# Block products: sums of weight blocks made one product sooner

## The chip, the cores and the metric

The kernel runs on one core of one Trainium2 chip. A core has five engines that work side by side, each through its own queue in order: TensorE (PE, matrix products; its weight loads are listed apart as PEld), VectorE (DVE), ScalarE (ACT), GpSimd (POOL) and SyncE (SP, which here only issues transfers). An engine that must wait for another stops at that instruction, and all behind it in its queue waits too. The metric is device time in microseconds, as the median of several executions; less is better.

## The reference, cut to what matters

One layer of a hybrid decoder: a feed-forward, a mixer (sparse attention beside a gated recurrence), a second feed-forward, and a final normalisation. 512 tokens, model width 1024, hidden width 2816, all in float32. The change concerns the two feed-forwards:

```python
def rmsnorm(x, g):
    y = x32 * lax.rsqrt(jnp.mean(x32 * x32, axis=-1, keepdims=True) + EPS)
    return (y * g.astype(jnp.float32)).astype(x.dtype)

def swiglu(x, w_gate, w_up, w_down):
    return (jax.nn.silu(x @ w_gate) * (x @ w_up)) @ w_down

x = x + 0.5 * swiglu(rmsnorm(x, ffn1_norm[l]), ffn1_wg[l], ffn1_wu[l], ffn1_wd[l])
...
x = x + 0.5 * swiglu(rmsnorm(x, ffn2_norm[l]), ffn2_wg[l], ffn2_wu[l], ffn2_wd[l])
```

## The kernel before, in words

**Number format.** A float32 operand is split into an upper half h (ACT rounds it by a copy to the type fp32r) and a lower half l (DVE subtracts h from the operand). A product of two split operands is three matmuls: h·h, h·l and l·h. For weights these tiles are called wh and wl, for hidden tiles hh and hl.

**Feed-forward.** `ffn_up` (L380) computes the gate and up projections of 22 hidden tiles of 128 rows. In the first feed-forward two tiles are done ahead of it and n0 is 2, in the second n0 is 0. The next DIRECT = 4 tiles (L47) are computed plainly, so that f0 = n0 + 4 hidden tiles come out before the block products: 6 in feed-forward 1, 4 in feed-forward 2.

**Block products.** The remaining tiles go in pairs. Two hidden tiles of one projection and the halves of the input and of the tokens form a 2x2 block product, done with seven half-size products instead of eight (a scheme of the Strassen kind). One such pair for one projection is called w here: there are count = 16 of them in feed-forward 1 and 18 in feed-forward 2; even w is the gate, odd w the up projection. The seven products need these weights: two halves of the tile x (products 1 and 2), a22 (4), s1 (5), s3 (7), and two sums that DVE makes: s2 = s1 + the first half of x (product 6), and s4 = s2 + the second half of x (product 3). s1 and s3 are themselves made by transfers: SyncE loads one block, and GpSimd issues a second transfer that adds another block to it (L444 to L451).

**The stream.** `stream` (L453 to L458) lists all products in the order in which PE runs them: 1 and 2 of w, 4 of w-1, 6 of w, 3 of w-1, 5 and 7 of w. It has 112 entries in feed-forward 1 and 126 in feed-forward 2. The order is written out by hand. For each product i the loop at L560 to L574 does this:

- `products(i)`: 12 matmuls on PE, each 128x256, that add into a PSUM tile. Products 1, 6, 7 and 4 of one w add to the same tile, beta, one after the other;
- `results(i - 1)`: after product 1, 6 and 7 ACT copies beta's present contents out to SBUF (tiles t1 and t2, shown as tg for the gate and tu for the up projection), and PE may go on adding to beta only then. DVE and ACT combine the parts into hidden tiles h;
- `prepare(i + 4)`: four products ahead (LEAD, L46), the weights of that product are made ready: the sum if it is product 6 or 3, then ACT's rounding (wh), then DVE's subtraction (wl). A pair of tiles wh, wl holds two products; there are three pairs;
- once in 14 products, while i // 14 < f0, `halve` (L577) splits one of the earlier hidden tiles into hh and hl for the down projection;
- once in 7 products, `load` (L436) asks for the weights of a later w; the raw tile x has three buffers, the blocks s1, s3, a22 and the sums s2, s4 come from 60 slots.

The first four products are made ready before the loop, while the plain tiles are computed (L543 to L545). Instructions that belong to a manual schedule keep this order; at its end the scheduler may mix in the first instructions of the down projection `ffn_down` (L584), whose order it chooses itself.

In the profile every instruction has the line of a helper (L174, or L162 for transfers), so that groups are told apart by their tiles. A product's matmuls read "cm" tiles (the prepared input) and wh or wl.

Of the kernel before, what the change touches and what calls it, by code (L numbers as in the profile page):

```python
# [10 lines left out]
F32R = mybir.dt.float32r  # L11
# [3 lines left out]
P = 128  # L15
# [30 lines left out]
LEAD = 4  # L46
# [133 lines left out]
def hybrid_kernel(ctx, tc, xt, vec, w1u, w1d, wm, wki, wrg, watt, wrnn, wout, w2u, w2d, out):  # L180
# [11 lines left out]
    wsp = ctx.enter_context(tc.tile_pool(name="wsp", bufs=3))  # L192
# [9 lines left out]
    def nm(s):  # L202
        cnt[0] += 1
        return f"{s}_{cnt[0]}"

    def slot(dt=F32, name="s"):
        return plan.take("slot", big.tile([P, S], dt, tag="slot", name=nm(name)))
# [7 lines left out]
    def psum(tag="mm"):  # L215
        return psp.tile([P, S], F32, tag=tag, name=nm(tag))
# [15 lines left out]
    WMAX = KD * P  # L232
# [6 lines left out]
    def wsplit(r, h, l):  # L239
        A.activation(h, r, AF.Copy)  # L240
        V.tensor_sub(l, r, f(h))

    def wload(src, cols):
        r, h, l = wtiles(cols)
        Q.dma_start(r, src)
        wsplit(r, h, l)
        return h, l
# [132 lines left out]
    def ffn_up(y, wu, n0, hs, g, waiting=(), given=()):  # L380
# [7 lines left out]
        H = KD // 2 * P  # L388
        f0 = n0 + DIRECT
        count = KF - f0  # L390
        ws = []
# [61 lines left out]
        stream = []  # L453
# [3 lines left out]
        w = count - 1  # L457
        stream[-3:] = [(5, w), (7, w), (3, w - 1), (4, w), (3, w)]  # L458
        units = []

        def prepare(i):
            p, w = stream[i]
            o = ws[w]
            if i % 2 == 0:
                units.append([wsp.tile([P, WMAX], F32R, tag=t, name=nm(t)) for t in ("wh", "wl")])
            h, l = (t[:, i % 2 * H:(i % 2 + 1) * H] for t in units[i // 2])
            if p == 6:
                o.s2 = slot(F32, "s2")
                V.tensor_add(o.s2, o.s1, o.x[:, :H])
            if p == 3:  # L470
                o.s4 = slot(F32, "s4")
                V.tensor_add(o.s4, o.s2, o.x[:, H:])
            wsplit({1: lambda: o.x[:, :H], 2: lambda: o.x[:, H:], 6: lambda: o.s2, 5: lambda: o.s1, 7: lambda: o.s3,
                    4: lambda: o.a22, 3: lambda: o.s4}[p](), h, l)

# [51 lines left out]
        with tc.manual_schedule(engines=ENGINES):  # L527
# [4 lines left out]
            for d, (n, j) in enumerate(direct):  # L532
                sums.append(psum(("aux", "mm")[n % 2]))
                if d == 1:
                    norm_rest(norm)
                    hs.extend(ffn_act(*p) for p in waiting)
                gemm(sums[d], split_[d], y, range(KD), last=False, upto=KD // 2)
                steps = [results_direct(d - 1)] if d else []
                if d + 2 < len(direct):
                    together(prepare_direct(), *steps)  # L540
                    fetch()
                else:
                    together(*steps)  # L543
                    for i in range(2):
                        prepare(2 * (d + 2 - len(direct)) + i)  # L545
                if d == 0:
                    for _ in range(3):
                        next(norm)
                if d in (4, 6):
                    load_ = load(len(ws))  # L550
                if d >= 4:
                    next(load_, None)
                if d > 1:
                    next(operands, None)
                gemm(sums[d], split_[d], y, range(KD), first=False, since=KD // 2)
                if d > 1:
                    next(operands, None)
            for _ in operands:
                pass
            for i in range(len(stream)):  # L560
                products(i)
                if i:
                    results(i - 1)
                else:
                    together(results_direct(len(direct) - 1))
                if i + LEAD < len(stream):
                    prepare(i + LEAD)
                else:
                    halve(hs, f0 + i + LEAD - len(stream))
                if i % 14 == 12 and i // 14 < f0:  # L570
                    halve(hs, i // 14)
                if i % 7 == 1 and len(ws) < count:
                    load_ = load(len(ws))
                next(load_, None)  # L574
# [61 lines left out]
    def given(r):  # L636
        h, l = (wsp.tile([P, WMAX], F32R, tag=t, name=nm(t)) for t in ("wh", "wl"))
        wsplit(r, h, l)
        return h, l
# [10 lines left out]
    pu, w = psum(), given(AH[0])  # L650
# [673 lines left out]
    for a, b in CHUNKS[:-1]:  # L1324
        w = wload(w2d[n, :, a * P:b * P], (b - a) * P)
# [3 lines left out]
    w = wload(w2d[n, :, a * P:b * P], (b - a) * P)  # L1329
# [32 lines left out]
    o = {}  # L1362
# [75 lines left out]
```

## Time and profile before

| What | us |
|---|---|
| median of 3 runs | 1103.74 (1102.88 to 1103.88) |
| the profiled execution | 1102.85 |
| its span, first to last instruction | 1101.1 |
| PE busy | 1081.7 |
| PE weight loads busy | 948.2 |
| DVE busy | 764.5 |
| ACT busy | 596.1 |
| POOL busy | 100.7 |

The stream of feed-forward 1 lies at about 73 to 238 us of the span, its down projection behind it to about 363; the mixer goes to about 734; the stream of feed-forward 2 lies at about 783 to 966. PE's granted clock is 0.995 of full speed over the span.

How to read the lines: an instruction is written as output tile <- input tiles, with shapes; a row of the timeline gives its start, its length, and in brackets how long its engine was idle before it and what ended that idle time. "A <- B: t, n, m" in the view of waits means that A waited t us in total for B, in n places, m at the longest. The chain that ended last is followed back from the last instruction of the program, at each step to what released it or to the instruction before it on its engine. "s" stands for a tile s1, s2, s3 or s4, since buffer numbers are left out.

### The profile page before, as it was taken

The page shows a single profiled execution, that of the slowest core. Times are in us where ns is not written, and L with a number is a line of the kernel's source. Part 1 is how long each engine was busy: PE and PEld are TensorE (multiplying, and loading weights), DVE is VectorE, ACT ScalarE, POOL GpSimd, SP SyncE. Part 2 cuts the span into 40 slices and gives each one's busy share as a digit, 9 for nine tenths or more (in the row PEclk, how much of TensorE's full clock was granted, in tenths as well). Part 3 has the DMA queues.
Part 4 walks back from the last instruction along what each step waited for, and adds up shares of the span by engine and source line. Part 5 has one row for each costly group of instructions (what it writes and reads, how often), then busy time and mean ns, then how long its engine had stood idle before and what let it go on. Part 6 is the DMA issues. An engine that isn't in the chain of part 4 may idle for free.

```text
span 1101.1 us, 16405 instructions
## 1 busy us (share of the span) xinstructions
PE 1081.7 (98%) x6184; PEld 948.2 (86%) x6184; DVE 764.5 (69%) x1376; ACT 596.1 (54%) x1093; POOL 100.7 (9%) x121
## 2 busy tenths in 40 slices
PE   9999999999999999999999999999999999999995
PEld 7889999998888777888888888888999999988885
DVE  6687777785333778999799868556877777773333
ACT  6665555564222558968885664346655555552220
POOL 0151111100000000000000000003411111000001
PEclk9999999999999999999999999999999999999998
DMA  7396677733333342232232203336967776543322
GB/s 269 83 242 183 159 180 194 162 106 102 102 90 102 116 134 81 83 98 85 77 96 83 81 30 99 112 115 155 218 156 190 191 159 179 122 133 93 96 63 77
DMA packets 61135, 140.22 MB, mean 127 GB/s; under 512 B 7168, under 2 KB 16512, under 8 KB 61056
## 3 DMA queue, kind: packets, MB, share of 16 engines
q1 hardware_dynamic: 45936, 116.58, 33.8%
q0 software_dynamic: 14976, 22.55, 13.4%
q8 instruction: 48, 0.79, 0.3%
q14 instruction: 31, 0.25, 0.1%
q10 hardware_dynamic: 144, 0.05, 0.0%
HBM read 130.24 MB, written 2.10 MB: 120 GB/s over the span
## 4 chain that ended last, share of the span: by engine, by line
PE 79%; DVE 9%; ACT 6%; DMA 3%; issue 3%; SPq 0%; DVEq 0%; ACTq 0%
PE mm L174 55%; PE aux L174 24%; DVE wl L174 3%; ACT wh L174 3%; DVE s L174 1%; DMA a<-w1u 1%; DMA gr<-wrg 1%; DVE tg L174 1%; ACT hh L174 1%; DVE yl L174 1%; ACT tg L174 0%; SPq L162 0%; DVE yf L174 0%; DMA wr<-w1u 0%; ACT cm L174 0%
## 5 line engine op out<-in xcount | busy, mean ns | idle before, releaser
L174 DVE TENSOR_TENSOR wl<-wr,wh 128x1024 fp32r<-128x1024 f32 (+3 forms) x204 | 193.0, 955 | 115.4 <-ACT wh L174 115.0
L174 ACT ACTIVATE wh<-wr 128x1024 fp32r<-128x1024 f32 (+4 forms) x206 | 171.2, 835 | 177.7 <-PE mm L174 67.1
L174 PE MATMUL mm<-cm,wh 128*128 128x256 f32 x1088 | 200.4, 284 | 2.5 <-ACT tg L174 2.5
L174 PEld LDWEIGHTS mm<-cm,wh 128*128 128x128 f32 x1088 | 169.7, 192 | 4.9 <-ACT tg L174 4.8
L174 PE MATMUL mm<-yh,wh 128*128 128x512 f32 (+1 forms) x416 | 164.7, 397 | 1.4 <-ACT yh L174 0.6
L174 PE MATMUL mm<-yl,wh 128*128 128x512 f32 (+1 forms) x416 | 163.3, 393 | 0.8 <-DVE yl L174 0.8
L174 PE MATMUL mm<-yh,wl 128*128 128x512 f32 x408 | 159.9, 392 | 0.0
L174 PE MATMUL mm<-cm,wl 128*128 128x256 f32 x544 | 153.9, 283 | 0.0
L174 PE MATMUL aux<-cm,wh 128*128 128x256 f32 x816 | 150.0, 283 | 0.0
L174 ACT ACTIVATE wh<-s 128x512 fp32r<-128x512 f32 x136 | 81.9, 626 | 101.7 <-DVE s L174 69.9
L174 DVE TENSOR_TENSOR wl<-s,wh 128x512 fp32r<-128x512 f32 x136 | 93.7, 690 | 52.9 <-ACT wh L174 50.6
L174 PEld LDWEIGHTS aux<-cm,wh 128*128 128x128 f32 x816 | 127.3, 192 | 0.0
L174 PE MATMUL aux<-cm,wl 128*128 128x256 f32 x408 | 115.5, 283 | 0.0
L174 PEld LDWEIGHTS mm<-cm,wl 128*128 128x128 f32 x544 | 104.3, 192 | 0.0
L174 PEld LDWEIGHTS mm<-yh,wh 128*128 128x128 f32 (+1 forms) x416 | 78.3, 188 | 19.2 <-ACT yh L174 1.9
L174 PEld LDWEIGHTS mm<-yl,wh 128*128 128x128 f32 (+1 forms) x416 | 78.0, 187 | 17.3 <-DVE yl L174 2.2
L174 PEld LDWEIGHTS mm<-yh,wl 128*128 128x128 f32 x408 | 77.0, 189 | 16.6 <-DVE wl L174 0.3
L174 PE MATMUL mm<-hh,wh 128*128 128x512 f32 (+1 forms) x206 | 78.8, 382 | 0.0
L174 PE MATMUL mm<-hl,wh 128*128 128x512 f32 (+1 forms) x206 | 78.5, 381 | 0.0
L174 PE MATMUL mm<-hh,wl 128*128 128x512 f32 (+1 forms) x206 | 78.4, 381 | 0.0
L174 PEld LDWEIGHTS aux<-cm,wl 128*128 128x128 f32 x408 | 78.3, 192 | 0.0
L174 PE MATMUL aux<-hh,wl 128*128 128x512 f32 x154 | 60.0, 390 | 0.0
(207 smaller groups left out, 1893.3 us busy)
## 6 DMA issues: line engine op xcount, KB each, us to landing
wr<-wm SPq DMA_DIRECT2D x39, 512.0 KB, 3.6
wr<-w2u SPq DMA_DIRECT2D x26, 512.0 KB, 3.7
wr<-w1u SPq DMA_DIRECT2D x21, 512.0 KB, 4.6
s<-w2u SPq DMA_DIRECT2D x36, 256.0 KB, 4.6
s<-w2u POOLq DMA_DIRECT2D x36, 256.0 KB, 5.4
s<-w1u SPq DMA_DIRECT2D x32, 256.0 KB, 5.1
s<-w1u POOLq DMA_DIRECT2D x32, 256.0 KB, 5.4
wr<-w1d SPq DMA_DIRECT2D x16, 448.0 KB, 3.3
```

The source lines that it names most:

```text
L174: return call(*args, **kw)
```

## The change

`prepare` made the sum for product 6 or 3 in the same step in which it also rounds and subtracts it. Now a function of its own, `add_weights`, makes it, and `prepare(i)` calls it for product i + 1, ahead of product i's own rounding and subtraction. The first LEAD = 4 products keep their sums where they were. On DVE the sum thus moves from just before its own subtraction to just before the subtraction of the product in front; between the two places lie the results of one product. The tile of the sum is taken from the slots one product sooner. The stream, the transfers as the program lists them and the number of instructions stay.

```diff
-        def prepare(i):
-            p, w = stream[i]
+        def add_weights(i):
+            p, w = stream[i] if i < len(stream) else (0, 0)
             o = ws[w]
-            if i % 2 == 0:
-                units.append([wsp.tile([P, WMAX], F32R, tag=t, name=nm(t)) for t in ("wh", "wl")])
-            h, l = (t[:, i % 2 * H:(i % 2 + 1) * H] for t in units[i // 2])
             if p == 6:
                 o.s2 = slot(F32, "s2")
                 V.tensor_add(o.s2, o.s1, o.x[:, :H])
             if p == 3:
                 o.s4 = slot(F32, "s4")
                 V.tensor_add(o.s4, o.s2, o.x[:, H:])
+
+        def prepare(i):
+            if i < LEAD:
+                add_weights(i)
+            if i + 1 >= LEAD:
+                add_weights(i + 1)
+            p, w = stream[i]
+            o = ws[w]
+            if i % 2 == 0:
+                units.append([wsp.tile([P, WMAX], F32R, tag=t, name=nm(t)) for t in ("wh", "wl")])
+            h, l = (t[:, i % 2 * H:(i % 2 + 1) * H] for t in units[i // 2])
             wsplit({1: lambda: o.x[:, :H], 2: lambda: o.x[:, H:], 6: lambda: o.s2, 5: lambda: o.s1, 7: lambda: o.s3,
                     4: lambda: o.a22, 3: lambda: o.s4}[p](), h, l)
```

## The prediction, made before the changed kernel was run

> **What bounds the kernel now.** I began with the page's busy table, then took the waits, the chain that ended last, and the timelines of ScalarE (ACT), VectorE (DVE) and TensorE (PE) around one repeating wait.
>
> ```profile
> span 1101.1 us, 16405 instructions
> PE 1081.7 (98%) x6184; PEld 948.2 (86%) x6184; DVE 764.5 (69%) x1376; ACT 596.1 (54%) x1093; POOL 100.7 (9%) x121
> ```
>
> TensorE is the bound, and 19.4 us of the span are left in which it does nothing. The change touches only the product streams of the two feed-forwards, so I looked for what PE waits for there.
>
> ```profile
> PEld mm L174 <- ACT tg L174: 4.8, 11, 0.4
> ...
> PE mm L174 <- ACT tg L174: 2.5, 11, 0.2
> ACT wh L174 <- DVE s L174: 69.9, 53, 2.9
> ```
>
> PE waits 11 times for one kind of ACT instruction, the copy of a partial result out of PSUM ("tg"). ACT waits much longer, 69.9 us, for DVE's sums of weight blocks ("s"), which is what the change moves. Whether the second feeds the first is shown by the whole chain, and then by the same view cut to one place. The columns are start, length, what.
>
> ```profile
> 76.58 1.69 PE mm L174 x12
> ...
> 95.77 1.70 PE mm L174 x12
> ...
> 116.42 1.70 PE mm L174 x12
> ...
> 199.02 1.70 PE mm L174 x12
> ...
> 210.80 2.88 PE aux L174 x24
> ...
> 220.88 2.88 PE aux L174 x24
> ...
> 805.03 1.70 PE mm L174 x12
> ...
> 866.97 1.70 PE mm L174 x12
> ```
>
> ```profile
> 93.52 0.69 DVE s L174
> ...
> 94.30 0.15 ACT wh L174
> ...
> 94.83 0.62 ACT hh L174
> 95.45 0.28 ACT tg L174
> ```
>
> Undisturbed, seven products take 220.88 - 210.80 = 10.08 us, so one product (12 matmuls) takes 1.44 and fourteen take 20.16. The rows of 1.70 us stand 116.42 - 95.77 = 20.65 apart. Each therefore costs 0.49 us. From 95.77 to 199.02 there are (199.02 - 95.77) / 20.65 = 5 steps, that is 6 such places in feed-forward 1. From 805.03 to 866.97 there are 3 steps, 4 places in feed-forward 2. These are exactly the iterations in which an earlier hidden tile is also halved ("hh", every 14 products, for f0 = 6 and 4 tiles). The eleventh wait, at 76.58, is the third product of feed-forward 1. The short chain names the cause: sum, rounding of the sum (wh), rounding of the hidden tile (hh), and only then the copy that PE needs.
>
> ACT and DVE at the first place:
>
> ```profile
> 88.94 0.63 ACT L174 ACTIVATE tg<-tg 128x512 f32<-128x512 f32 x1 [1.09 <-DVE tg L174]
> 89.48 0.62 ACT L174 ACTIVATE wh<-a 128x512 fp32r<-128x512 f32 x1
> 91.45 0.63 ACT L174 ACTIVATE wh<-s 128x512 fp32r<-128x512 f32 x1 [1.36 <-DVE s L174]
> 91.99 0.37 ACT L174 ACTIVATE tu<-mm 128x256 f32<-128x256 f32 x1
> 94.30 0.63 ACT L174 ACTIVATE wh<-s 128x512 fp32r<-128x512 f32 x1 [1.94 <-DVE s L174]
> 94.83 0.62 ACT L174 ACTIVATE hh<-h 128x512 fp32r<-128x512 f32 x1
> 95.36 0.37 ACT L174 ACTIVATE tg<-mm 128x256 f32<-128x256 f32 x1
> ```
>
> ```profile
> 88.49 0.42 DVE L174 SCALAR_TENSOR_TENSOR tg<-aux,tg 128x256 f32<-128x256 f32 x1
> 90.12 0.69 DVE L174 TENSOR_TENSOR wl<-a,wh 128x512 fp32r<-128x512 f32 x1 [1.22 <-ACT wh L174]
> 90.73 0.69 DVE L174 TENSOR_TENSOR s<-s,wr 128x512 f32<-128x512 f32 x1
> 92.12 0.69 DVE L174 TENSOR_TENSOR wl<-s,wh 128x512 fp32r<-128x512 f32 x1 [0.70 <-ACT wh L174]
> 92.73 0.42 DVE L174 TENSOR_TENSOR tu<-aux,tu 128x256 f32<-128x256 f32 x1
> 93.18 0.43 DVE L174 TENSOR_TENSOR h<-tu,tg 128x256 f32<-128x256 f32 x1
> 93.52 0.68 DVE L174 TENSOR_TENSOR s<-s,wr 128x512 f32<-128x512 f32 x1
> ```
>
> ```profile
> 95.26 0.28 PE L174 MATMUL mm<-cm,wl 128*128 128x256 f32 x1
> 95.77 0.50 PE L174 MATMUL mm<-cm,wh 128*128 128x256 f32 x2 [0.23 <-ACT tg L174]
> ```
>
> Products are numbered from 0, as in the code; the one at 95.77 is 15. Matmuls start 0.12 apart (1.44 / 12), so it was due at 95.38. Counting back, product 14 began at 93.94, 13 at 92.50, 12 at 91.06. A product's last matmul runs 0.28, so its result is there 0.16 after the next one begins: 11's at 91.22, 12's at 92.66. The copy at 95.36 reads product 12, so it could have run 2.7 us sooner. It stood behind wh and hh, which stood behind the sum at 93.52, which stood behind DVE's wait for ACT at 92.12. The two engines take turns waiting for each other.
>
> **The change, part by part.**
>
> *The moved sums.* There are 2 x 16 in feed-forward 1 and 2 x 18 in feed-forward 2. One in each lies among the first four products and stays, so 66 move and none is added. At 0.68 us each, 45 us of DVE work change place. I replay the rows above with the new order. In the iteration of product 10 the first sum now follows the row at 88.49: 88.85 to 89.5, while DVE waits for ACT anyway (1.22 idle before 90.12), so "wl<-a" stays at 90.12 and the sum costs nothing. Without that cover it would put 0.6 us (90.73 to 90.12) on all DVE work behind it. ACT rounds the sum right behind "wh<-a", at about 90.0 instead of 91.45. DVE makes the second sum at 90.73, the lower half at 91.35, tu at 91.95, h at 92.4. ACT copies tu at 91.26 when product 11 is out, rounds the second sum at 91.55 (it is there at about 91.4), hh at 92.1, and the copy tg follows product 12 at 92.7. It ends near 93.1. PE needs it at 95.38, so 2.3 us are in hand and the wait goes. What is late next on ACT is only the result of PE itself.
>
> *Sum.* 10 waits x 0.49 = 4.9 us. The eleventh stays: the copy at its head comes in the first iterations, ahead of any moved sum.
>
> *Two other readings of the same waits.* The matmul row gives 10/11 of 2.5 = 2.3 us, the weight loads' row 10/11 of 4.8 = 4.4 us. The distance of starts is the measure with nothing modelled in it, and I take 4.9. The Trainium skill, Perfetto Trace Analysis, section "Identifying the Most-Contended Engine", says that matmul busy time is a bad measure of TensorE's headroom because pipelined instructions look smaller in the trace, and that weight-load busy time should be used. By the one row the time would be 1101.4, by the other 1099.3; the trace agrees with the page, since 4.4 is near the 4.9 of the starts and 2.3 is not.
>
> *Sums wait for an accumulating transfer one product sooner.*
>
> ```profile
> s<-w1u POOLq DMA_DIRECT2D x32, 256.0 KB, 5.4
> ```
>
> ```profile
> 70.96 2.11 POOL L162 DMA_DIRECT2D s<-w1u  x2
> ```
>
> ```profile
> 79.85 0.69 DVE L174 TENSOR_TENSOR s<-s,wr 128x512 f32<-128x512 f32 x1
> ```
>
> The tightest is the first moved sum, at 79.85, where DVE was not idle; it would now start near 79.0. Its transfer was issued from 70.96 and lands 5.4 later at the median, 76.4. If it landed only at 79.85, DVE would stand 0.9 us once, and the product behind it (the eighth, begun near 76.58 + 5 x 1.44 = 83.8) would still have its weights. I take 0.
>
> *Buffers.* The raw tile is read for the last time by the second sum, so SyncE may issue the next loads about 1.4 us sooner. PE waits for no DMA in the streams, so that gains nothing; GpSimd's accumulating loads follow them and get sooner too. The slots of s2 and s4 are taken one product sooner out of 60. In the order of the instructions no late new releaser shows; I take 0.
>
> *The seam to the down projection.* The scheduler orders the last iterations anew: on DVE and ACT the first three splits of down weights come after one or two other instructions, and PE runs the first output tile for 16 matmuls straight where five matmuls of the second tile stood.
>
> ```profile
> 239.17 1.22 DVE L174 TENSOR_TENSOR wl<-wr,wh 128x1024 fp32r<-128x1024 f32 x1 [0.79 <-ACT wh L174]
> ...
> 246.03 0.69 DVE L174 TENSOR_TENSOR hl<-h,hh 128x512 fp32r<-128x512 f32 x1
> ```
>
> ```profile
> 246.18 0.39 PE L174 MATMUL aux<-hh,wh 128*128 128x512 f32 x1
> ```
>
> The lower half of 246.03 is done at 246.72; it would be needed 0.23 (one matmul) after 246.18, so PE would wait 0.3 us, and perhaps 0.7 again a few tiles on, if DVE were no sooner: 1.0 per feed-forward, 2.0 in all. Against it, DVE idles 0.79 before 239.17 and ACT's part of that comes from a late sum, so both should be over 0.8 us earlier. In the other direction, PE has no gap here to gain. I take 0 and keep 2.0 for the range.
>
> **The sum** against the profiled execution: 1102.85 (span 1101.1 and 1.75 around it) less 4.9 is 1097.95. The median of the runs, 1103.74, is 0.89 above that execution, so I forecast 1103.74 - 4.9 = 1098.8.
>
> **Rivals.**
>
> *Half.* The matmul row is right, or the copy stays late in some places: 2.3 us, 1101.4. For it: PE's own idle time. Against it: the step of 20.65. Chance 0.06.
>
> *No change: the gap is one of buffers.* The split weights have three pairs of buffers, and a regular gap could be the wait for one; then sums made sooner wait for their buffer instead: 1103.7. Against it: "wh<-s" at 94.30 takes the buffer of products 10 and 11, and "tu<-mm" at 91.99 already read product 11, so the buffer was free 2.3 us before. The Trainium skill, the same page, section "Optimization Strategy", says that the same gap repeating can mean too little SBUF or PSUM for the next tile; by that rule this rival holds, and the trace disagrees. Chance 0.04.
>
> *Slower: the sum ahead of the subtraction.* On DVE each moved sum now stands in front of the lower half of an earlier product. Where DVE does not wait for ACT, that half and all behind it are 0.6 us late, and at a product boundary PE pays 0.49 as above. It decides once the lower halves are ready less than 0.6 us ahead of PE. Here "wl<-a" ends at 90.81 for product 14, begun at 93.94: 3.1 us in hand. If it came in each of the 33 weight pairs it would cost 33 x 0.49 = 16.2, less 4.9: 1115.0. Chance 0.06.
>
> *The seam loses* its 2.0: 1100.8, chance 0.04. The forecast has 0.80.
>
> **How the numbers follow.** A run of this kernel can tell about 0.2% (2.2 us) from no change. Faster by more than that: forecast, seam and half of "half", 0.87; within it, 0.07; slower, 0.06. The range goes from 1097.7 (0.9 below for the spread of the runs, 1102.88 to 1103.88, and for the eleventh wait) to 1101.5 (the seam's bound and "half"), which leaves out the last two signs, about 1 in 10.
>
> **What would show it.** In the profile after, PE's wait for "ACT tg" should count 1 instead of 11; starts fourteen products apart should be 20.16 apart in both streams; ACT's wait for "DVE s" should fall from 69.9 to under 10, and in its place ACT waits for PE; DVE's busy time should stay at 764. The forecast is wrong if new PE waits for "DVE wl" appear in the streams, or gaps after about 243 and 970 at the seams.

## The result, and the profile after

| | before | changed |
|---|---|---|
| median, us | 1103.06 (1102.27 to 1103.88, 5 runs) | 1097.68 (1096.5 to 1098.07, 5 runs) |
| ratio to before | 1 | 0.9949, 95% interval 0.9935 to 0.9962 |
| span of the profiled execution, us | 1101.1 | 1096.2 |

The changed kernel is faster by 5.4 us in the medians and by 4.9 us between the two profiled executions. The forecast was 4.9 us, and 1098.8 us with a range that began at 1097.7. The ratios here and below, with their 95% intervals, are worked out from all executions and are not exactly the quotients of the medians.

The view of waits of the changed kernel, its lines for PE first, then ACT's wait for the sums:

```profile
PE aux L174 <- ACT rl L174: 1.7, 2, 1.1
PE aux L174 <- DVE last L174: 1.5, 1, 1.5
PE aux L174 <- DVE cc L174: 1.1, 1, 1.1
PE mm L174 <- DVE yl L174: 0.8, 2, 0.6
...
PE aux L174 <- DMA cm<-cb: 0.2, 1, 0.2
```

```profile
ACT wh L174 <- DVE s L174: 30.9, 17, 2.0
```

PE no longer waits for "ACT tg"; the 11 places are gone, and one wait for a transfer has come at the head of a stream. ACT waits 30.9 us for sums instead of 69.9. The whole chain (start, length, what) shows where the time went:

```profile
24.18 5.01 PE mm L174 x22
...
70.54 5.84 DMA cm<-cb
76.94 1.45 PE mm L174 x12
...
94.23 2.88 PE mm L174 x24
97.11 2.88 PE aux L174 x24
...
117.27 2.88 PE aux L174 x24
...
235.35 11.81 PE mm L174 x52
...
737.82 9.79 PE aux L174 x48
...
961.79 11.81 PE mm L174 x52
...
1089.26 1.58 DVE o L174 x4
```

117.27 - 97.11 = 20.16: fourteen products now take what fourteen undisturbed products took before. The same points in the whole chain of before:

```profile
24.06 5.01 PE mm L174 x22
...
238.16 8.19 PE mm L174 x36
...
740.79 9.77 PE aux L174 x48
...
966.59 6.23 PE mm L174 x27
...
1094.13 1.58 DVE o L174 x4
```

By stage: up to the end of the first stream 214.10 against 211.17, 2.93 gained (6 x 0.49 = 2.94 was forecast); the down projection and the mixer 0.16; up to the end of the second stream 225.80 against 223.97, 1.83 gained (4 x 0.49 = 1.96); the rest 0.07; the start gave back 0.12. The sum is 4.87. PE's granted clock reads 1.00 in both streams of both profiles, and fourteen undisturbed products take the same 20.16 us in both, so the clock has no part in what the streams gained.

The timelines of ACT and DVE at the place that the prediction replayed; all times stand 0.12 later here:

```profile
89.60 0.62 ACT L174 ACTIVATE wh<-a 128x512 fp32r<-128x512 f32 x1
90.12 0.62 ACT L174 ACTIVATE wh<-s 128x512 fp32r<-128x512 f32 x1
91.39 0.38 ACT L174 ACTIVATE tu<-mm 128x256 f32<-128x256 f32 x1 [0.65 <-PE mm L174]
91.67 0.62 ACT L174 ACTIVATE wh<-s 128x512 fp32r<-128x512 f32 x1
92.19 0.62 ACT L174 ACTIVATE hh<-h 128x512 fp32r<-128x512 f32 x1
92.83 0.38 ACT L174 ACTIVATE tg<-mm 128x256 f32<-128x256 f32 x1
```

```profile
88.94 0.68 DVE L174 TENSOR_TENSOR s<-s,wr 128x512 f32<-128x512 f32 x1
90.25 0.69 DVE L174 TENSOR_TENSOR wl<-a,wh 128x512 fp32r<-128x512 f32 x1 [0.62 <-ACT wh L174]
90.86 0.68 DVE L174 TENSOR_TENSOR s<-s,wr 128x512 f32<-128x512 f32 x1
91.46 0.68 DVE L174 TENSOR_TENSOR wl<-s,wh 128x512 fp32r<-128x512 f32 x1
```

The copy tg starts at 92.83 instead of 95.36. The sum at 88.94 fills part of DVE's wait for ACT (0.62 left of 1.22), and "wl<-a" is as early as before, 90.25 against 90.12 + 0.12.

### The profile page after: what moved, and what is told of

Same layout as the page of the kernel before. It is cut to its first block, busy times and chain, and to the rows that moved or that the text cites. A ratio compares the mean times of both kernels' runs of the same rounds, so it can differ in the third digit from the quotient of the medians.

```text
span 1096.2 us, 16417 instructions
## 1 busy us (share of the span) xinstructions
PE 1079.5 (98%) x6184; PEld 948.4 (87%) x6184; DVE 763.6 (70%) x1376; ACT 598.8 (55%) x1093; POOL 100.6 (9%) x121
## 4 chain that ended last, share of the span: by engine, by line
PE 88%; DVE 6%; ACT 3%; issue 1%; DMA 1%; SPq 0%; DVEq 0%; ACTq 0%; POOLq 0%
PE mm L174 60%; PE aux L174 29%; DVE wl L174 1%; ACT wh L174 1%; DVE yl L174 1%; DMA cm<-cb 1%; ACT L174 0%; DVE yf L174 0%; DVE ca L174 0%; DMA x<-xt 0%; DVE xc L174 0%; ACT rl L174 0%; DVE h L174 0%; DVE o L174 0%; ACT yh L174 0%
## 5 line engine op out<-in xcount | busy, mean ns | idle before, releaser
L174 ACT ACTIVATE wh<-s 128x512 fp32r<-128x512 f32 x136 | 83.0, 623 | 38.9 <-DVE s L174 30.9
L174 PE MATMUL aux<-hl,wh 128*128 128x512 f32 x154 | 60.0, 389 | 0.0
```

The source lines that it names most:

```text
L174: return call(*args, **kw)
```

## The experiments

Theory: the gain is ten PE waits of 0.49 us. Each comes from one chain, at the ten places where two iterations in a row each make a sum and the second also rounds a hidden tile: DVE and ACT alternate, and the copy that PE needs stands behind them. Rivals: the gain is spread over the moved sums; the sums ahead of the subtractions cost something; the half microsecond beyond 4.9 is a second gain.

All kernels ran in 5 rounds beside the kernel before (4 to 11 executions of each), whose medians there were 1102.42 us (first four) and 1102.74 us (last four). The variants of the changed kernel replace the test on LEAD by a condition:

```diff
+        def sooner(j):
+            return LEAD <= j < len(stream) and CONDITION
...
-            if i < LEAD:
+            if not sooner(i):
                 add_weights(i)
-            if i + 1 >= LEAD:
+            if sooner(i + 1):
                 add_weights(i + 1)
```

**The changed kernel again** (no edit).

> The changed kernel once more beside the kernel before. Theory: ten waits of 0.49 us and nothing else, 4.9 us, a ratio of 0.9956; the half microsecond that the first measurement gave beyond that (5.4 us, 0.9949) is scatter of the runs, and the profiled spans differ by 4.9. Rival: another 0.5 us or more is really gained elsewhere; then the ratio stays at 0.995 or below and the span falls by more than 5.3.

1097.98 us, ratio 0.9964 (0.9951 to 0.9978), span 1096.2. The gain is 4.4 us here and was 5.4 in the first measurement; 4.9 lies in both intervals, and the span is the same. Nothing speaks for a second gain.

**All sums but those of the ten places.**

```diff
+            CONDITION: not ((j - LEAD) % 14 in (11, 12) and (j - LEAD) // 14 < f0)
```

> All sums sooner except the two (s2 and s4) of each of the ten halving iterations: 46 of 66 moved. Theory: the chain sum, rounding, rounding of the hidden tile, copy is whole again in each of the ten places; PE waits 10 or 11 times for the copy, and the time is that of the kernel before (ratio 1.000). Rival (the gain is spread over all moved sums): 46/66 of 5.4 us, 3.8 us, ratio 0.9966.

1103.22 us, ratio 1.0005 (0.9997 to 1.0014). The waits in its profile:

```profile
PE mm L174 <- ACT tg L174: 2.3, 10, 0.2
...
PEld mm L174 <- ACT tg L174: 4.3, 10, 0.4
```

With 46 of the 66 sums moved nothing is gained, and PE waits ten times for the copy. The gain lies in those ten places.

**Only ten sums.**

```diff
+            CONDITION: (j - LEAD) % 14 == 12 and (j - LEAD) // 14 < f0
```

> Only ten sums sooner: s4 in each of the ten halving iterations. Theory, replayed from the rows of before at the first place: the second sum at 90.7, the first at 91.4, its rounding at 92.1, the copy tu at 92.6, the rounding of the second sum at 92.9, the hidden tile at 93.4, the copy tg ends near 94.3; PE needs it at 95.38, so the wait goes and the whole 4.9 us are gained (ratio 0.9956). Rival (spread): 10/66 of 5.4 us, 0.8 us, ratio 0.9993.

1098.04 us, ratio 0.9962 (0.9950 to 0.9975): the whole gain from 10 of 66 sums. PE's one wait for the copy that is left is the one at the third product of feed-forward 1. The view of waits has ACT waiting longer for the sums than before the change, at no cost:

```profile
PE mm L174 <- ACT tg L174: 0.2, 1, 0.2
```

```profile
ACT wh L174 <- DVE s L174: 79.2, 54, 2.9
```

The replay had the two sums in the wrong order. s2 stands first here, and ACT rounds it while DVE makes s4. The copy tg started at 92.91, or 93.3 on the clock of before, whose stream began 0.41 later; I had it at 93.9.

**The halving moved, no sum moved.** This is an edit of the kernel before.

```diff
-                if i % 14 == 12 and i // 14 < f0:
-                    halve(hs, i // 14)
+                if i % 14 == 0 and 0 < i // 14 <= f0:
+                    halve(hs, i // 14 - 1)
```

> The kernel before with no sum moved; the halving of a hidden tile stands two iterations later in each period of 14, where no sum is made. Theory: without the 0.5 us of the hidden tile's rounding ahead of it the copy starts at about 94.8 and ends at 95.2, before PE needs it at 95.38; at the new place ACT has no copy to make, so PE does not wait and 4.9 us are gained (ratio 0.9956), perhaps 0.5 less if the margin of 0.2 us does not hold everywhere. Rival (it is the sums themselves that hold PE): nothing is gained, ratio 1.000.

1097.38 us, ratio 0.9960 (0.9948 to 0.9972). The same gain without touching a sum. ACT at the first place (its stream began 0.35 earlier than that of before), and ACT's wait for the sums:

```profile
93.97 0.63 ACT L174 ACTIVATE wh<-s 128x512 fp32r<-128x512 f32 x1 [1.94 <-DVE s L174]
94.51 0.36 ACT L174 ACTIVATE tg<-mm 128x256 f32<-128x256 f32 x1
```

```profile
ACT wh L174 <- DVE s L174: 105.8, 64, 3.3
```

The rounding still waits 1.94 us for the sum, but nothing stands between it and the copy, and that is enough: the copy ends at 94.87, or 95.22 on the clock of before, and PE needs it at 95.38. ACT's total wait for sums is half as large again as before, and the time is as good as the best. In these kernels the size of that wait says nothing of the time.

**Only s2, only s4.**

```diff
+            CONDITION (s2): stream[j][0] == 6
+            CONDITION (s4): stream[j][0] == 3
```

> Only the sums s2 (product 6) sooner, 32 of 66. Theory: s2 ahead shortens the alternation of the two engines before s4, so the whole gain comes from it alone: replayed, s4 at 92.4, its rounding at 93.1, the hidden tile at 93.7, the copy ends near 94.5, 0.9 before PE needs it; ratio 0.996. Rival (each half of the sums carries its share): 32/66 of the gain, ratio 0.998.

> Only the sums s4 (product 3) sooner, 34 of 66. Theory: the whole gain again, as the ten s4 alone gave it; ratio 0.996. Rival (shares): ratio 0.998.

1098.36 us, 0.9961 (0.9947 to 0.9974), and 1098.21 us, 0.9958 (0.9945 to 0.9970). Each half of the change gives all of it. The gain is no sum of shares: the chain need only be shortened once, by more than the 0.5 us that PE waited.

**Moved sums made twice and three times.** The result stays the same; N is 2 or 3.

```diff
-                V.tensor_add(o.s2, o.s1, o.x[:, :H])
+                for _ in range(N if i >= LEAD else 1):
+                    V.tensor_add(o.s2, o.s1, o.x[:, :H])
```

(and so for s4)

> The changed kernel with each moved sum made twice, the second writing the same result: 66 sums of 0.6 us more on DVE, 40 us in all. It prices the rival 'the sum ahead of the subtraction'. Theory: DVE has 165 - 129 = 36 us idle in the stream of feed-forward 1 and takes 31 x 0.6 = 19 more; the subtraction and the copy come 0.6 to 1.2 us later and 2.3 us are in hand; no PE wait, time that of the changed kernel (ratio 0.996). Rival: lower halves late at the 33 pairs, up to 16 us more, ratio 1.011.

> Each moved sum made three times: 132 sums of 0.6 us more, 79 us. Theory: in the stream of feed-forward 1 DVE would have 129 + 37 = 166 us of work for 161 us of PE, so DVE becomes the bound there and PE waits for wl; a loss of 3 to 10 us per stream against the changed kernel, ratio 1.002 to 1.015. Rival: still hidden, ratio 0.996.

Twice: 1097.94 us, ratio 0.9956 (0.9943 to 0.9968), nothing lost. ACT there, first place; its stream lies about 0.8 later than that of before (its first matmul starts at 74.10 against 73.34):

```profile
93.01 0.63 ACT L174 ACTIVATE wh<-s 128x512 fp32r<-128x512 f32 x1 [0.61 <-DVE s L174]
93.54 0.62 ACT L174 ACTIVATE hh<-h 128x512 fp32r<-128x512 f32 x1
94.06 0.36 ACT L174 ACTIVATE tg<-mm 128x256 f32<-128x256 f32 x1
```

The copy ends at 94.42 and PE starts product 15 at 96.13, with no wait, so 1.7 us are left of the changed kernel's margin of 2.3. Three times: 1124.74 us, ratio 1.0202 (1.0188 to 1.0216), a loss of 27 us against the changed kernel; I had expected 6 to 20. Waits, and one of the places on PE:

```profile
PE mm L174 <- ACT tu L174: 21.5, 16, 1.7
```

```profile
108.42 0.50 PE L174 MATMUL mm<-cm,wh 128*128 128x256 f32 x2 [1.66 <-ACT tu L174]
130.50 0.51 PE L174 MATMUL mm<-cm,wh 128*128 128x256 f32 x2 [1.67 <-ACT tu L174]
```

DVE at that place, ahead of the wait:

```profile
101.40 2.14 DVE L174 TENSOR_TENSOR s<-s,wr 128x512 f32<-128x512 f32 x3
103.45 0.68 DVE L174 TENSOR_TENSOR wl<-a,wh 128x512 fp32r<-128x512 f32 x1
104.05 2.14 DVE L174 TENSOR_TENSOR s<-s,wr 128x512 f32<-128x512 f32 x3
106.11 0.68 DVE L174 TENSOR_TENSOR wl<-s,wh 128x512 fp32r<-128x512 f32 x1
106.71 0.42 DVE L174 TENSOR_TENSOR tg<-aux,tg 128x256 f32<-128x256 f32 x1
```

What the rival "the sum ahead of the subtraction" feared, DVE work that comes too late for PE, thus does come, but only between one and two extra sums for each moved one. That DVE would be the bound was right: in those 22.08 us (130.50 - 108.42) it is busy for 20.64, and the chain that ended last runs mostly along its sums and lower halves there. But PE does not wait for the lower halves (wl), as I wrote: it is once more the copy out of PSUM that it waits for, behind ACT, behind DVE, in 16 places, one in 14 products. The step there is 22.08 us against 20.16 in the ten periods in which a hidden tile is also halved; later in feed-forward 2 it is 21.47. This run adds work to DVE and does not test the order of the same work.

## Where the prediction was right, and the terms that failed

*What bounds, and the sum.* Right. 10 x 0.49 = 4.9 against 4.87 between the profiles, stage by stage. The median fell by 5.4 in the first measurement and by 4.4 in the second; the five other kernels in which these waits are gone and nothing new came lie 4.4 to 5.0 below the kernel before (0.9956 to 0.9962). The mechanism is the one that was forecast.

*How the numbers follow.* This is the step that failed: the two terms that turn the gain into a time, the base and the spread. 1097.68 lies 0.02 us below 1097.7, the lower end, and 1.16 below the forecast. Of that, 0.68 is the base: the forecast started from 1103.74, the median of three executions, which with five is 1103.06 (and beside the experiments 1102.42 and 1102.74). The other 0.48 is the gain in the medians, 5.38 against 4.9, which the repeat, with 4.4, does not confirm. The prediction had a nearer base: the one profiled execution, 1102.85, gave it 1097.95. The spread was too small as well. 0.9 came from those three executions, between 1102.88 and 1103.88, while the same changed program ran between 1096.34 and 1099.25 in ten; and the lower end stands only 1.1 below the forecast, so about 0.2 is left for the eleventh wait, which by the distance of starts is 0.44 (78.10 - 74.78 = 3.32 for two products that undisturbed take 2.88). Either term alone, put right, would have held the result; that it missed by 0.02 and not by more, or not at all, is chance.

What makes one execution of the same program 2.9 us longer than another was not tried. The runs show what it goes with: the spans of the ten are 1096.2 to 1097.4 us at a mean granted clock of 0.994, 1095.9 to 1096.2 at 0.995, 1094.7 to 1095.5 at 0.996, and 1094.6 at 0.997. Between the clock and the time no cause is shown.

*The other readings.* The matmul row (2.3) was wrong, the weight loads' row (4.4) and the distance of starts (4.9) near. The Trainium skill, Perfetto Trace Analysis, section "Identifying the Most-Contended Engine", says this of busy shares, that the matmul row is a poor measure of the headroom and the weight loads' row a better one. Carried over to these waits, the trace agrees: 4.87 was gained.

*The moved sums.* The replay of the first place was right to 0.05 us (copy at 92.83 - 0.12 = 92.71 against 92.7). That ACT's wait for sums would fall under 10 us was wrong: it is 30.9, in 17 places of up to 2.0. Fifteen of them, of 1.98 each, are the iterations after an odd w's product 3, where even the sooner sum stands on DVE behind that product's results. They cost PE nothing. The other signs held: DVE is busy for 763.6 us against 764.5, ACT's copies tg and tu wait 72.8 us for PE instead of 14.4, and PE has no wait for "DVE wl".

*The eleventh wait.* It was to stay. In the profile after, PE waits at that place for a transfer of the prepared input (cm<-cb) one product sooner, and the copy is then in time; in the changed kernel's second profile the wait for the copy is there again. First the one profile, then the other:

```profile
76.43 0.39 PE L174 MATMUL aux<-cm,wh 128*128 128x256 f32 x1 [0.17 <-DMA cm<-cb]
```

```profile
77.06 0.51 PE L174 MATMUL mm<-cm,wh 128*128 128x256 f32 x2 [0.20 <-ACT tg L174]
```

The second and third product together take 3.33 us in the one and 3.34 in the other, against 3.32 before, so the place costs the same either way; which of the two is late differs between two executions of the same program.

*Transfers and buffers.* Taken as 0; no wait of PE or DVE for a weight transfer is among the waits of the streams.

*The seam.* Taken as 0, with 2.0 at risk; right. PE's work there moved by 2.81 us (235.35 against 238.16). On DVE the lower half of the 1024-column chunk moved with it, by 2.71 (236.46 against 239.17), and the lower half that PE was to wait for by 4.02 (242.01 against 246.03), 1.2 more than PE. PE shows no gap there.

```profile
236.46 1.21 DVE L174 TENSOR_TENSOR wl<-wr,wh 128x1024 fp32r<-128x1024 f32 x1
...
242.01 0.68 DVE L174 TENSOR_TENSOR hl<-h,hh 128x512 fp32r<-128x512 f32 x1
```

*Rivals.* "Half" is ruled out by the profiles. "A gap of buffers" is ruled out by the kernel with the halving moved, which takes the weight buffers in the same order and has none of the ten gaps; the Trainium skill, the same page, section "Optimization Strategy", offers the lack of buffers as one possible reading of a repeating gap, and here it was another. "Slower" did not occur with one sum, nor with two; with three sums, which is more work and not only another order, PE lost 27 us.

## What to carry to other kernels

A small repeating wait of the bounding engine is worth its step, the distance of starts with and without it, times its count; follow the chain back to the copy, load or buffer release that it stands for, and look which instructions stand ahead of that one in its queue. Here any single shortening of that chain by more than the wait took all of the gain, and further ones took nothing more: ten sums, either kind of sum, or an unrelated instruction moved out of the way all gave the same 4.4 to 5 us. The large waits between two other engines (69.9 us here) are no measure of what can be gained: of the kernels with the whole gain, one had 30.9 and one 105.8. And a forecast of a time needs a base and a spread from more than three executions, even where the gain itself is right to a few hundredths of a microsecond.

## What the runs showed of the hardware that I had not expected

Sums repeated into the same tile take more of DVE than their neighbours: the step from a single sum to the next instruction is 0.60 us (90.86 to 91.46), from three to the next 2.05 us (101.40 to 103.45), that is 0.72 for each added one. Three sums for one thus put 2 x 0.72 = 1.4 us on the queue, which is probably part of why the loss at three was larger than expected from 0.6 each. The mean granted clock goes with the span in the ten executions of the changed kernel, as shown above, but not in every kernel: with the halving moved, two executions at 0.994 took 1095.6 and 1097.9 us, and two at 0.997 took 1095.6 and 1095.9.
